# Attention scores: K in one tile per head, a sample block padded to 128 queries and 640 keys

## Chip, cores and metric

The kernel runs on one core of one Trainium2 chip. The metric is the device time of one execution in microseconds, as the median of several runs. The core's engines are TensorE (PE), VectorE (DVE), ScalarE (ACT), GpSimd (POOL) and SyncE (SP), which issues most DMAs.

## What is computed

One inference step of a two-layer streaming encoder: layer 0 is a Mamba-2 mixer with a SwiGLU feed-forward part, layer 1 a banded attention with another one. 1024 prompt frames and 64 sample frames go through both. The change lies in the attention of layer 1, 16 heads of 64:

```python
def band_attend(q, k, v, qpos, kpos, rel_bias):
    dist = jnp.clip(qpos[:, None] - kpos[None, :], -REL_CLIP, REL_CLIP) + REL_CLIP
    bias = rel_bias[:, dist].astype(jnp.float32)
    qc = qpos // CHUNK
    kc = kpos // CHUNK
    valid = (kpos[None, :] >= 0) & (kc[None, :] <= qc[:, None]) & (kc[None, :] >= qc[:, None] - BAND_CHUNKS)
    s = jnp.einsum('bqhd,bkhd->bhqk', q, k).astype(jnp.float32) * (ATT_HEAD_DIM ** -0.5) + bias
    s = jnp.where(valid, s, -jnp.inf)
    p = jax.nn.softmax(s, axis=-1).astype(v.dtype)
    return jnp.einsum('bhqk,bkhd->bqhd', p, v)
```

Chunks are of 64 frames, and a query sees its own chunk and the eight before it. The sample's 64 queries see 512 cached keys and their own 64.

## The kernel before

All activations lie transposed, features on the 128 partitions and the 1088 frames (1024 + 64) along the free dimension, in three slices of 384, 384 and 320 frames (`SL`). Matrix products are made in units: `unit` runs one 128-wide column block of weights over one slice, as 8 steps of three matmuls (`passes`, L454 to L456: weights and activations are each split into a high and a low float32r part). PE's order is the order in which the program emits its instructions. A `Stream` with a clock of its own, `st.t`, decides it: units advance the clock, and side tasks (the attention blocks among them) are let in between the quarters of a unit when their due times have come. The other engines' orders, SP's and POOL's DMA queues among them, are made by the compiler from priorities (`high_priority`) and dependences.

The attention goes by 8 pairs of heads (j = 0 to 7). For each pair, units make K, V and Q of each slice: `evk` (L1569), `evv` (L1623) and `evq` (L1589) take a unit's result from PSUM. K is scaled into `kf` and split for each of the two heads e into a tile whose one half of the partitions holds the high part and whose other half the low part (L1581 on ScalarE, L1582 on DVE). There are five buffers (`KBUF`) of 384 columns for each head, one for each slice of K; Q has two buffers for each of its four parts. A score is then two matmuls over 128 partitions, one with the high part of Q (L1675) and one with the low part (L1676).

`att_task(j, b)` handles block b of 9: blocks 0 to 7 are 128 prompt queries each against up to 640 keys (128 keys for block 0, 256, 384 and 512 for blocks 1 to 3, 640 from block 4 on), block 8 is the 64 sample queries against 576 keys. Stage A makes the scores. Since K lies in slices, they come in pieces (`pcs_`): 384+128 in block 3, 384+256 in blocks 4 and 7, 256+384 in block 5, 128+384+128 in block 6, and 512 (cached, `Ck`) + 64 in block 8. Pieces that fit together go into the same bank of a PSUM tile `S` of two banks. For each bank DVE then adds the bias and takes the row minimum of the negated scores (L1685), ScalarE makes the exponentials and their sum (L1690), and DVE divides (L1691, L1692). Stage B, later, transposes the probabilities by 128 keys on PE (L1707, tile `ptp`, in the same ring of two PSUM buffers as `S`) and copies them to `pT`, for head 0 on DVE and for head 1 on ScalarE (L1712; for block 8 the last 64 keys in a copy of their own, L1714). Stage C, `values` (L1728), multiplies V with them (L1746); after three blocks the output goes to `oscr` (L1754, L1755).

V of a slice is transposed by three 128-column matmuls in `v_task` (L1615) and copied to `Vn` (L1617, and L1619 for the sample's 64 rows). The bias of a pair is loaded for each head as a band of 128 by 640 (`load_bias`, L1555); POOL writes the mask into two of its corners (L1561, L1562). A unit waits until the blocks that read the oldest K, V or Q slices are emitted (`free_q`, L1766).

Of the kernel before, what the change touches and what calls it, by code (L numbers as in the profile page):

```python
# [374 lines left out]
def hybrid_kernel(  # L375
# [1148 lines left out]
    with ExitStack() as es:  # L1524
# [7 lines left out]
        def load_pair(j):  # L1532
            kqv[j] = dict(K={}, Q={}, V={})
# [32 lines left out]
        def k_tiles():  # L1566
            return [sb2.tile([P, 384], F32R, tag=f"K{e}", bufs=KBUF, name=f"K{e}") for e in range(2)]

        def evk(j):  # L1569
            d = kqv[j]  # L1570

            def f(s, p_):
# [5 lines left out]
                Kd = d["K"].get(s) or k_tiles()  # L1578
                for e in range(2):

                    A.copy(Kd[e][H2[e], :n], kf[H2[e], :n])  # L1581
                    V.tensor_tensor(Kd[e][H2[1 - e], :n], kf[H2[e], :n], Kd[e][H2[e], :n], op=ALU.subtract)  # L1582
                d["K"][s] = Kd
# [5 lines left out]
        def evq(j):  # L1589
            def f(s, p_):  # L1590
# [3 lines left out]
                kqv[j]["Q"][s] = Q  # L1594
                qf = sb2.tile([P, 384], F32, tag="kqv", bufs=2, name="qf")
# [14 lines left out]
        def v_task(j, s, vt):  # L1610
            Vn = kqv[j]["V"][s] = sb2.tile([P, 3, P], F32, tag="Vn", bufs=KBUF, name="Vn")
            pt = ax("vtp")
            for i in range(3):
                L = CHL[3 * s + i]
                PE.transpose(pt[:L, i * P:(i + 1) * P], vt[:, i * P:i * P + L], ident)  # L1615
            nf = 3 if s < 2 else 2
            V.tensor_copy(Vn[:, :nf, :], pt[:, :nf * P].rearrange("p (a b) -> p a b", b=P))  # L1617
            if s == 2:
                V.tensor_copy(Vn[:64, 2, :], pt[:64, 256:384])  # L1619
            yield 0.33, 0  # L1620
            v_done.append((j, s))

        def evv(j):  # L1623
            def f(s, p_):
# [6 lines left out]
                if s == 2:  # L1631
                    nc.sync.dma_start(vT_o[j * P:(j + 1) * P, 256:576], vt[:, :320])
# [5 lines left out]
        def att_task(j, b):  # L1638
# [9 lines left out]
            pcs_ = []  # L1648
            if b < 8:
                k0 = max(0, b - 4)  # L1650
                w_ = P * (b + 1 - k0)
                for t_ in range(3):
                    c0, c1 = max(k0, 3 * t_), min(b + 1, 3 * t_ + 3)
                    if c0 < c1:
                        pcs_.append((d["K"][t_], (c0 - 3 * t_) * P, (c1 - c0) * P))
            else:
                k0 = 0
                w_ = 576
                pcs_ = [(d["Ck"], 0, 512), (d["K"][2], 256, 64)]
            parts, bank, fill = [], 0, 0  # L1660
            for kd_, ko, fw in pcs_:
                if fill + fw > 512:
                    bank, fill = bank + 1, 0
                parts.append((bank, fill, kd_, ko, fw))
                fill += fw
            split = sum(p_[4] for p_ in parts if p_[0] == 0)
            nkt = (w_ + P - 1) // P
            sts = []
            for e in range(2):
                sp = psS.tile([P, 2, 512], F32, tag="S", name="S")  # L1670
                qs = slice(i * P, i * P + L)
                qh, ql = d["Q"][s][e]
                for bank, f0, kd_, ko, fw in parts:
                    dst = sp[:L, bank, f0:f0 + fw]
# [5 lines left out]
                brev = bt[:L, 0:w_][:, ::-1] if b < 8 else bt[:L, 64:640][:, ::-1]  # L1680

                low = TOP
                with tc.high_priority(ATP):
                    for pi, (f0, f1) in enumerate([(0, split)] + ([(split, w_)] if split < w_ else [])):
                        V.tensor_tensor_reduce(  # L1685
                            out=sc[:L, f0:f1], in0=sp[:L, pi, :f1 - f0], in1=brev[:, f0:f1],
                            scale=-1.0, scalar=low, op0=ALU.add, op1=ALU.min, accum_out=mx[:L, pi:pi + 1],
                        )
                        low = mx[:L, pi:pi + 1]
                    A.activation(sc[:L, :w_], sc[:L, :w_], AF.Exp, bias=low, scale=-1.0, accum_out=mx[:L, 3:4])  # L1690
                    V.reciprocal(mx[:L, 3:4], mx[:L, 3:4])  # L1691
# [293 lines left out]
```

## Time and profile before

| | us |
|---|---|
| median of 3 runs | 2992.34 |
| lowest, highest | 2991.45, 2995.91 |
| the profiled execution | 2995.14 |
| its span, first to last instruction | 2993.4 |
| mean granted PE clock | 0.993 |
| first score to last value matmul | 1659.1 to 2151.0 |

The profile is of one execution. In its lists, an instruction's row gives the start and the duration in us, the engine, the line of the kernel, the operation, what it writes and reads (tile names without buffer numbers), the shapes (for a matmul first the partitions and columns of the stationary operand, then those of the moving one), how many such instructions are merged in the row, and in brackets the idle time of the engine before it with what ended that. A row of the waits names who waited for whom, then the us in total, how often, and the longest. PE's matmuls are pipelined, and their ends are modelled. In a row with three durations these are the shortest, the median and the longest in ns.

### The profile page before, as it was taken

How to read it: one execution, taken by the hardware profiler on the slowest of the kernel's cores; microseconds unless marked ns; L12 is line 12 of the kernel's file. 1: busy time of each engine (PE TensorE's matmuls, PEld its weight loads, DVE VectorE, ACT ScalarE, POOL GpSimd, SP SyncE). 2: the span in 40 equal slices, each digit the busy share in tenths (PEclk: the TensorE clock that was granted, in tenths of full speed). 3: DMA queues.
4: the chain of work that ended last, by engine and by line, in shares of the span. 5: the costliest groups of instructions: out<-in, count | busy, mean ns of one | idle time of the engine just before them, and what ended most of it. 6: DMA issues, size and time to landing. Idle time of an engine off the chain costs nothing.

```text
span 2993.4 us, 56388 instructions
## 1 busy us (share of the span) xinstructions
PE 2935.9 (98%) x21626; PEld 2878.7 (96%) x21626; DVE 2039.4 (68%) x4471; ACT 1450.9 (48%) x2574; POOL 709.0 (24%) x821
## 2 busy tenths in 40 slices
PE   8899999999999999999999999999999999999999
PEld 7899999999999999999999899999999999999999
DVE  7788887876768554574557777777778655475544
ACT  6675666654453232244445566555654322244443
POOL 1233333330121433351111000000131343452111
PEclk9999999999999999999999999999999999999999
DMA  3333333334654222255655322222356222245654
GB/s 122 99 108 95 103 98 105 95 102 150 187 147 144 84 73 80 76 161 173 203 177 168 88 83 73 69 65 85 123 166 187 80 75 77 80 149 174 214 180 136
DMA packets 201550, 363.36 MB, mean 121 GB/s; under 512 B 20544, under 2 KB 149280, under 8 KB 201280
## 3 DMA queue, kind: packets, MB, share of 16 engines
q1 hardware_dynamic: 199488, 353.39, 38.1%
q0 software_dynamic: 1792, 6.36, 1.1%
q8 instruction: 170, 2.79, 0.4%
q14 instruction: 100, 0.82, 0.1%
HBM read 292.47 MB, written 62.74 MB: 119 GB/s over the span
## 4 chain that ended last, share of the span: by engine, by line
PE 83%; DVE 9%; DMA 4%; ACT 2%; issue 2%; POOL 0%; SPq 0%; DVEq 0%; ACTq 0%; POOLq 0%
PE px L1263 9%; PE px L1265 9%; PE px L1264 9%; PE mm L454 7%; PE mm L456 7%; PE mm L455 7%; PE po L1463 6%; PE po L1464 6%; PE po L1462 6%; PE mmx L455 3%; PE mmx L454 3%; PE mmx L456 3%; PE po L1746 2%; PE ptp L1707 1%; PE yp L884 1%
## 5 line engine op out<-in xcount | busy, mean ns | idle before, releaser
L454 PE MATMUL mm<-r,hl 128*128 128x384 f32 (+2 forms) x1664 | 557.9, 335 | 5.5 <-ACT BT L768 3.0
L456 PE MATMUL mm<-r,hl 128*128 128x384 f32 (+2 forms) x1664 | 540.3, 325 | 3.6 <-DVE hl L353 2.8
L455 PE MATMUL mm<-r,hl 128*128 128x384 f32 (+2 forms) x1664 | 539.2, 324 | 0.0
L341 DVE TENSOR_TENSOR hl<-raw,hl 128x1024 fp32r<-128x1024 f32 (+1 forms) x219 | 260.9, 1192 | 222.6 <-ACT hl L340 218.6
L1264 PE MATMUL px<-r,hl 128*128 128x288 f32 (+1 forms) x1184 | 347.6, 294 | 0.0
L454 PEld LDWEIGHTS mm<-r,hl 128*128 128x128 f32 x1664 | 316.1, 190 | 7.5 <-ACT BT L768 3.2
L456 PEld LDWEIGHTS mm<-r,hl 128*128 128x128 f32 x1664 | 315.2, 189 | 5.0 <-DVE hl L353 3.9
L455 PEld LDWEIGHTS mm<-r,hl 128*128 128x128 f32 x1664 | 316.5, 190 | 0.1
L1263 PE MATMUL px<-r,hl 128*128 128x288 f32 x1056 | 310.9, 294 | 0.0
L1265 PE MATMUL px<-r,hl 128*128 128x288 f32 x1056 | 310.7, 294 | 0.0
L340 ACT CAST hl<-raw 128x1024 fp32r<-128x1024 f32 (+1 forms) x219 | 219.9, 1005 | 177.5 <-PE po L1464 101.6
L480 POOL TENSOR_TENSOR ssum<-ssum,sq 128x256 f32<-128x256 f32 (+3 forms) x97 | 130.4, 1345 | 639.3 <-ACT sq L479 622.5
L1264 PEld LDWEIGHTS px<-r,hl 128*128 128x128 f32 x1184 | 222.6, 188 | 0.0
L1265 PE MATMUL px<-rx,hl 128*128 128x256 f32 x768 | 216.2, 282 | 4.5 <-DVE hl L341 4.5
L1263 PE MATMUL px<-rx,hl 128*128 128x256 f32 x768 | 216.7, 282 | 2.3 <-ACT hl L340 2.3
L1463 PE MATMUL po<-rx,hl 128*128 128x384 f32 (+1 forms) x624 | 201.6, 323 | 0.1
L1263 PEld LDWEIGHTS px<-r,hl 128*128 128x128 f32 x1056 | 198.4, 188 | 0.1
L1265 PEld LDWEIGHTS px<-r,hl 128*128 128x128 f32 x1056 | 198.3, 188 | 0.0
L1462 PE MATMUL po<-rx,hl 128*128 128x384 f32 (+1 forms) x608 | 197.4, 325 | 0.1
L1464 PE MATMUL po<-rx,hl 128*128 128x384 f32 (+1 forms) x608 | 196.5, 323 | 0.0
L1264 PE MATMUL px<-rx,hl 128*128 128x256 f32 x640 | 179.8, 281 | 0.0
L290 POOL TENSOR_TENSOR tt<-raw 128x512 f32<-128x512 f32 x40 | 56.0, 1399 | 439.3 <-DMA raw<-in_w_f_dram 362.9
(359 smaller groups left out, 8116.0 us busy)
## 6 DMA issues: line engine op xcount, KB each, us to landing
raw<-in_w_f_dram SPq DMA_DIRECT2D x154, 512.0 KB, 3.8
rx<-in_w_f_dram SPq DMA_DIRECT2D x54, 512.0 KB, 3.7
raw<-in_w_in_dram SPq DMA_DIRECT2D x40, 512.0 KB, 3.7
MT<-ascr SPq DMA_DIRECT2D x48, 384.0 KB, 3.8
sg<-hscr SPq DMA_DIRECT2D x88, 192.0 KB, 3.3
raw<-in_w_f_dram SPq DMA_DIRECT2D x44, 384.0 KB, 3.3
raw<-in_w_so_dram SPq DMA_DIRECT2D x32, 512.0 KB, 3.8
raw<-in_w_kv_dram SPq DMA_DIRECT2D x18, 512.0 KB, 3.5
```

The lines of the kernel that those rows point to most:

```text
L340: self.nc.scalar.copy(h, v)
L341: (eng or self.eng or self.nc.vector).tensor_tensor(lo, v, h, op=ALU.subtract)
L454: PE.matmul(ps[:, :n], h_, xh, start=(first and i == 0), stop=False)
L455: PE.matmul(ps[:, :n], h_, xl, start=False, stop=False)
L456: PE.matmul(ps[:, :n], l_, xh, start=False, stop=(last and i == nk - 1))
L480: (eng or G).tensor_tensor(ssum[:, :n], ssum[:, :n], q[:, :n], op=ALU.add)
L1263: PE.matmul(ps, wh, ah[:, k, :], start=(k == 0), stop=False)
L1264: PE.matmul(ps, wh, al[:, k, :], start=False, stop=False)
L1265: PE.matmul(ps, wl, ah[:, k, :], start=False, stop=(k == 3))
L1462: PE.matmul(ps[:, :n], wh, xh, start=(k == 0), stop=False)
L1463: PE.matmul(ps[:, :n], wh, xl, start=False, stop=False)
L1464: PE.matmul(ps[:, :n], wl, xh, start=False, stop=(k == FT - 1))
```

## The change

K of a pair lies in one tile of 9*128 columns per head, with two buffers. Its columns from 1088 on, Q's columns from 320 on in the last slice, and V's columns from 320 on in the last slice are filled with zeros by POOL. The scores of blocks 0 to 3 are made in one piece, those of blocks 4 to 7 in two halves of 320, and block 8 is taken with 128 queries and 640 keys, as 512 cached keys and a piece of 128. Its transposes, copies, reductions and exponentials are of full size; its values keep their 64 queries, but run over the 128 rows of the last piece. Block 8's bias is read from column 0 on, so that the existing mask corner covers the 64 keys that don't exist. The due times of block 8's stages are computed with 640 in place of 576. The diff:

```diff
@@ -1530,7 +1530,7 @@
         pos = {}
 
         def load_pair(j):
-            kqv[j] = dict(K={}, Q={}, V={})
+            kqv[j] = dict(K=set(), Kt=[], Q={}, V={})
 
         def load_side(j):
             d = kqv[j]
@@ -1563,9 +1563,6 @@
                 bias.append(bt)
             kqv[j]["bias"] = bias
 
-        def k_tiles():
-            return [sb2.tile([P, 384], F32R, tag=f"K{e}", bufs=KBUF, name=f"K{e}") for e in range(2)]
-
         def evk(j):
             d = kqv[j]
 
@@ -1575,12 +1572,15 @@
                 kf = sb2.tile([P, 384], F32, tag="kqv", bufs=2, name="kf")
                 with tc.high_priority(HIP):
                     V.tensor_tensor(kf[:, :n], p_[:, :n], rba[s][:, :n], op=ALU.mult)
-                Kd = d["K"].get(s) or k_tiles()
-                for e in range(2):
-
-                    A.copy(Kd[e][H2[e], :n], kf[H2[e], :n])
-                    V.tensor_tensor(Kd[e][H2[1 - e], :n], kf[H2[e], :n], Kd[e][H2[e], :n], op=ALU.subtract)
-                d["K"][s] = Kd
+                if not d["Kt"]:
+                    d["Kt"] = [sb2.tile([P, 9 * P], F32R, tag=f"K{e}", bufs=2, name=f"K{e}") for e in range(2)]
+                    for Kd in d["Kt"]:
+                        G.memset(Kd[:, T:].bitcast(F32), 0.0)
+                for e, Kd in enumerate(d["Kt"]):
+                    hi, lo = Kd[H2[e], 384 * s:384 * s + n], Kd[H2[1 - e], 384 * s:384 * s + n]
+                    A.copy(hi, kf[H2[e], :n])
+                    V.tensor_tensor(lo, kf[H2[e], :n], hi, op=ALU.subtract)
+                d["K"].add(s)
                 if s:
                     a_, b_, c_ = (128, 384, 0) if s == 1 else (0, 320, 256)
                     nc.sync.dma_start(kT_o[j * P:(j + 1) * P, c_:c_ + b_ - a_], kf[:, a_:b_])
@@ -1592,6 +1592,9 @@
 
                 Q = [[sb2.tile([P, 384], F32R, tag=f"Q{x}{e}", bufs=2, name=f"Q{x}{e}") for x in "hl"] for e in range(2)]
                 kqv[j]["Q"][s] = Q
+                if s == 2:
+                    for q_ in Q[0] + Q[1]:
+                        G.memset(q_[:, n:].bitcast(F32), 0.0)
                 qf = sb2.tile([P, 384], F32, tag="kqv", bufs=2, name="qf")
                 with tc.high_priority(HIP):
                     V.scalar_tensor_tensor(qf[:, :n], p_[:, :n], 0.125, rba[s][:, :n], op0=ALU.mult, op1=ALU.mult)
@@ -1611,12 +1614,8 @@
             Vn = kqv[j]["V"][s] = sb2.tile([P, 3, P], F32, tag="Vn", bufs=KBUF, name="Vn")
             pt = ax("vtp")
             for i in range(3):
-                L = CHL[3 * s + i]
-                PE.transpose(pt[:L, i * P:(i + 1) * P], vt[:, i * P:i * P + L], ident)
-            nf = 3 if s < 2 else 2
-            V.tensor_copy(Vn[:, :nf, :], pt[:, :nf * P].rearrange("p (a b) -> p a b", b=P))
-            if s == 2:
-                V.tensor_copy(Vn[:64, 2, :], pt[:64, 256:384])
+                PE.transpose(pt[:, i * P:(i + 1) * P], vt[:, i * P:(i + 1) * P], ident)
+            V.tensor_copy(Vn, pt[:, :3 * P].rearrange("p (a b) -> p a b", b=P))
             yield 0.33, 0
             v_done.append((j, s))
 
@@ -1629,6 +1628,7 @@
                 if s == 1:
                     nc.sync.dma_start(vT_o[j * P:(j + 1) * P, 0:256], vt[:, 128:384])
                 if s == 2:
+                    G.memset(vt[:, n:], 0.0)
                     nc.sync.dma_start(vT_o[j * P:(j + 1) * P, 256:576], vt[:, :320])
                 st.spawn(v_task(j, s, vt), 3.0 if j else 5.0)
             return f
@@ -1645,51 +1645,40 @@
             )
             L = CHL[b]
 
-            pcs_ = []
             if b < 8:
                 k0 = max(0, b - 4)
                 w_ = P * (b + 1 - k0)
-                for t_ in range(3):
-                    c0, c1 = max(k0, 3 * t_), min(b + 1, 3 * t_ + 3)
-                    if c0 < c1:
-                        pcs_.append((d["K"][t_], (c0 - 3 * t_) * P, (c1 - c0) * P))
+                half = w_ if w_ <= 512 else w_ // 2
+                parts = [(c_ // half, d["Kt"], k0 * P + c_, half) for c_ in range(0, w_, half)]
             else:
-                k0 = 0
-                w_ = 576
-                pcs_ = [(d["Ck"], 0, 512), (d["K"][2], 256, 64)]
-            parts, bank, fill = [], 0, 0
-            for kd_, ko, fw in pcs_:
-                if fill + fw > 512:
-                    bank, fill = bank + 1, 0
-                parts.append((bank, fill, kd_, ko, fw))
-                fill += fw
-            split = sum(p_[4] for p_ in parts if p_[0] == 0)
-            nkt = (w_ + P - 1) // P
+                k0, w_, half = 0, WIN, 512
+                parts = [(0, d["Ck"], 0, 512), (1, d["Kt"], 8 * P, P)]
+            nkt = w_ // P
             sts = []
             for e in range(2):
                 sp = psS.tile([P, 2, 512], F32, tag="S", name="S")
-                qs = slice(i * P, i * P + L)
+                qs = slice(i * P, (i + 1) * P)
                 qh, ql = d["Q"][s][e]
-                for bank, f0, kd_, ko, fw in parts:
-                    dst = sp[:L, bank, f0:f0 + fw]
+                for bank, kd_, ko, fw in parts:
+                    dst = sp[:, bank, :fw]
                     PE.matmul(dst, qh[:, qs], kd_[e][:, ko:ko + fw], start=True, stop=False)
                     PE.matmul(dst, ql[:, qs], kd_[e][:, ko:ko + fw], start=False, stop=True)
                 sc = late["sb3"].tile([P, WIN], F32, tag="sc", bufs=4, name="sc")
                 mx = late["sb3"].tile([P, 4], F32, tag="mx", bufs=4, name="mx")
                 bt = d["bias"][e]
-                brev = bt[:L, 0:w_][:, ::-1] if b < 8 else bt[:L, 64:640][:, ::-1]
+                brev = bt[:, 0:w_][:, ::-1]
 
                 low = TOP
                 with tc.high_priority(ATP):
-                    for pi, (f0, f1) in enumerate([(0, split)] + ([(split, w_)] if split < w_ else [])):
+                    for pi, (f0, f1) in enumerate([(0, half)] + ([(half, w_)] if half < w_ else [])):
                         V.tensor_tensor_reduce(
-                            out=sc[:L, f0:f1], in0=sp[:L, pi, :f1 - f0], in1=brev[:, f0:f1],
-                            scale=-1.0, scalar=low, op0=ALU.add, op1=ALU.min, accum_out=mx[:L, pi:pi + 1],
+                            out=sc[:, f0:f1], in0=sp[:, pi, :f1 - f0], in1=brev[:, f0:f1],
+                            scale=-1.0, scalar=low, op0=ALU.add, op1=ALU.min, accum_out=mx[:, pi:pi + 1],
                         )
-                        low = mx[:L, pi:pi + 1]
-                    A.activation(sc[:L, :w_], sc[:L, :w_], AF.Exp, bias=low, scale=-1.0, accum_out=mx[:L, 3:4])
-                    V.reciprocal(mx[:L, 3:4], mx[:L, 3:4])
-                    V.tensor_scalar(sc[:L, :w_], sc[:L, :w_], mx[:L, 3:4], None, op0=ALU.mult)
+                        low = mx[:, pi:pi + 1]
+                    A.activation(sc[:, :w_], sc[:, :w_], AF.Exp, bias=low, scale=-1.0, accum_out=mx[:, 3:4])
+                    V.reciprocal(mx[:, 3:4], mx[:, 3:4])
+                    V.tensor_scalar(sc[:, :w_], sc[:, :w_], mx[:, 3:4], None, op0=ALU.mult)
                 sts.append(sc)
             cur["A"] = seqn + 1
             cur["t"] = st.t + 1.1 * w_ / 640 + GAP_A
@@ -1703,15 +1692,11 @@
                 pT = late["sb3"].tile([P, 5, P], F32, tag="pT", bufs=6, name="pT")
                 pt = psS.tile([P, 2, 512], F32, tag="S", name="ptp").rearrange("p a b -> p (a b)")
                 for kt in range(nkt):
-                    kw = min(P, w_ - kt * P)
-                    PE.transpose(pt[:kw, kt * P:kt * P + L], sts[e][:L, kt * P:kt * P + kw], ident[:L, :L])
+                    PE.transpose(pt[:, kt * P:(kt + 1) * P], sts[e][:, kt * P:(kt + 1) * P], ident)
                 ptv = pt[:, :640].rearrange("p (a b) -> p a b", b=P)
-                nfull = w_ // P
                 cpf = A.copy if e else V.tensor_copy
                 with tc.high_priority(ATP):
-                    cpf(pT[:, :nfull, :L], ptv[:, :nfull, :L])
-                    if nfull < nkt:
-                        cpf(pT[:64, nfull, :L], ptv[:64, nfull, :L])
+                    cpf(pT[:, :nkt, :L], ptv[:, :nkt, :L])
                 PTs.append(pT)
             cur["B"] = seqn + 1
             cost += 1.1 * w_ / 640
@@ -1735,16 +1720,15 @@
                     pos["po"] = ax("po")
                 po = pos["po"]
                 for kt in range(nkt):
-                    kw = min(P, w_ - kt * P)
                     for e in range(2):
                         if 3 * s + i < 8:
                             vs = d["V"][(k0 + kt) // 3][:, (k0 + kt) % 3, 64 * e:64 * e + 64]
                         elif kt < 4:
                             vs = d["Cv"][:, kt, 64 * e:64 * e + 64]
                         else:
-                            vs = d["V"][2][:64, 2, 64 * e:64 * e + 64]
+                            vs = d["V"][2][:, 2, 64 * e:64 * e + 64]
                         PE.matmul(
-                            po[64 * e:64 * e + 64, i * P:i * P + L], vs, PTs[e][:kw, kt, :L],
+                            po[64 * e:64 * e + 64, i * P:i * P + L], vs, PTs[e][:, kt, :L],
                             start=(kt == 0), stop=(kt == nkt - 1),
                         )
                 if i == 2:
@@ -1808,7 +1792,6 @@
                 if s and w is wv:
                     W.put()
 
-        kqv[0]["K"][2] = k_tiles()
         units(W.get(), 1, evk, (0, 1))
         W.put()
         st.wait_for(lambda: 2 in done)
```

## The prediction

> **What bounds the kernel now.** I read the page's engine shares first, then the engines over the attention stage alone, then what TensorE (PE) waited for there, and last the order of instructions in one head pair.
>
> ```profile
> PE 2935.9 (98%) x21626; PEld 2878.7 (96%) x21626; DVE 2039.4 (68%) x4471; ACT 1450.9 (48%) x2574; POOL 709.0 (24%) x821
> ```
>
> ```profile
> 1655.00:2150.00 495.00, 480.30 (x3873) 455.15 (x3871) 385.69 (x1212) 294.85 (x730) 5.32 (x31) 1.00 0.26 77
> ```
>
> ```profile
> PE ptp L1707 <- DVE mx L1685: 4.8, 9, 1.9
> PE S L1675 <- DVE pT L1712: 4.4, 11, 0.6
> ```
>
> The first line says that PE is busy for 98% of the whole span. The second is the stretch 1655 to 2150 us, in which all scores of the change lie: after the length come the busy times of PE, weight load, DVE, ACT and POOL, then the granted clock, 1.00. PE works 480.30 of 495.00 us, so it bounds this stage too; DVE has 385.69, 78%, and POOL almost nothing. The last two lines are the waits in that stretch that involve the edited lines: 4.8 us in all of the transposes for the score reduction, and 4.4 us of the scores for a copy of transposed probabilities. Whatever the change does to other stages is at most a shift of memory addresses. So the sum is made of PE time in the score, transpose and value steps of 8 head pairs, and of what these waits make of it. Times of starts matter here, not durations: PE's matmuls overlap, and what one costs is the time until the next starts.
>
> **Scores of block 3 (keys 0 to 511), from 384+128 to one 512.** Per head (e = 0, 1) the block issues a high and a low matmul for each piece.
>
> ```profile
> 1801.02 0.34 PE L1675 MATMUL S<-K,Qh 128*128 128x384 f32 x1
> ...
> 1802.11 0.39 PE L454 MATMUL mm<-r,hl 128*128 128x384 f32 x1
> 1802.34 0.34 PE L455 MATMUL mm<-r,hl 128*128 128x384 f32 x1
> ```
>
> The eight matmuls take 1802.11 - 1801.02 = 1.09 us, and the one after them lasts 0.23 instead of 0.17 us (0.17 is the step of a 384 in the middle of a unit), so 1.15 us. Four matmuls of 512 come instead, priced by the sample block's:
>
> ```profile
> 1775.86 0.45 PE L1675 MATMUL S<-Ck,Qh 128*64 128x512 f32 x1 [0.37 <-DVE pT L1712]
> ...
> 1776.47 0.42 PE L1675 MATMUL S<-Ck,Qh 128*64 128x512 f32 x1
> 1776.72 0.39 PE L1676 MATMUL S<-Ck,Ql 128*64 128x512 f32 x1
> 1776.95 0.19 PE L1675 MATMUL S<-K,Qh 128*64 128x64 f32 x1
> ...
> 1777.04 0.55 PE L1615 MATMUL vtp<-ident,vt 128*128 128x128 f32 x3
> ```
>
> A 512 steps 1776.95 - 1776.72 = 0.23 us, so four take 0.92: a gain of 0.23 us per pair. For this same step the Trainium skill (TensorE: Matmul & The Clock Gate, section Back-to-back issue gap) gives about 131 ns per 512-column matmul in a sustained stream; by it the four would take 0.52 us and the gain of this block would be 0.63 us per pair, an estimate from that page. The rows above, 0.23 and 0.25 us, do not agree with it, and the sum goes by the rows.
>
> **Scores of block 6, from 128+384+128 to 320+320.**
>
> ```profile
> 1819.85 0.22 PE L1675 MATMUL S<-K,Qh 128*128 128x128 f32 x1
> ...
> 1821.21 0.22 PE L1675 MATMUL S<-K,Qh 128*128 128x128 f32 x1
> ...
> 1821.38 0.39 PE L454 MATMUL mm<-r,hl 128*128 128x384 f32 x1
> ```
>
> ```profile
> 1782.35 0.31 PE L456 MATMUL mm<-r,hl 128*128 128x320 f32 x1
> ...
> 1783.67 0.31 PE L456 MATMUL mm<-r,hl 128*128 128x320 f32 x1
> ```
>
> Now 1821.38 - 1819.85 = 1.53 us, and again about 0.06 in the matmul behind it: 1.59. A 320 steps (1783.67 - 1782.35)/9 = 0.147 us, as the second fence holds the first and last of ten of them, so eight take 1.18: a gain of 0.41 us per pair. Blocks 4, 5 and 7 go from 384+256 to 320+320, the same number of matmuls and of columns, and I cost them at nothing; blocks 0 to 2 stay as they are.
>
> **The sample block (8): scores, transposes, values.** The first 512 after the wait stays. Each head's two 64-column pieces, 1777.04 - 1776.95 = 0.09 us, become two of 128, which took 1821.38 - 1821.21 = 0.17 us at the end of block 6; and what follows a pair of 128 steps up to 0.06 us longer. So two heads cost 0.16 to 0.28 us more; I take 0.20. For the transposes:
>
> ```profile
> 1783.91 0.82 PE L1707 MATMUL ptp<-ident,sc 64*128 64x64 f32 x10
> 1784.65 0.42 PE L454 MATMUL mm<-r,hl 128*128 128x320 f32 x1
> ```
>
> ```profile
> 1804.08 0.34 PE L456 MATMUL mm<-r,hl 128*128 128x384 f32 x1
> 1804.25 0.82 PE L1707 MATMUL ptp<-ident,sc 128*128 128x128 f32 x6
> 1804.82 0.42 PE L454 MATMUL mm<-r,hl 128*128 128x384 f32 x1
> ```
>
> ```profile
> 2145.71 1.31 PE L1707 MATMUL ptp<-ident,sc 128*128 128x128 f32 x10
> ```
>
> From the last unit matmul before to the first after, ten half-size transposes take 1784.65 - 1783.67 = 0.98 us; six full ones take 1804.82 - 1804.08 = 0.74. Ten full ones last 1.31 where six last 0.82, so four more are up to 0.49, and ten would be 1.23 us at most; with the bare column ratio they would be near 1.15. I take 0.20 us more per pair, between 0.17 and 0.25.
>
> ```profile
> 1788.84 0.64 PE L1746 MATMUL po<-pT,Cv 128*64 128x64 f32 x16
> 1789.40 0.33 PE L1746 MATMUL po<-pT,Vn 64*64 64x64 f32 x4
> 1789.67 0.44 PE L1707 MATMUL ptp<-ident,sc 128*128 128x128 f32 x2
> ```
>
> The values keep 64 queries. Today 16 matmuls take 0.56 us and the 4 of half height 0.27. Made full height they should go at the rate of the 16, 0.035 each, so 0.14: 0.13 us less. How they hand over to the next instruction isn't in the trace, so the bounds are 0 and 0.13 and I take 0.10.
>
> **The sum on PE** is -0.23 - 0.41 + 0.20 + 0.20 - 0.10 = -0.34 us per pair, -2.7 us over 8.
>
> **What the wait does with it.** Block 6's scores stand ahead of one of the waits of the first section. Its rows:
>
> ```profile
> 1821.18 0.55 DVE L1602 TENSOR_TENSOR Ql<-qf,Qh 64x384 fp32r<-64x384 f32 x1 [0.58 <-ACT Qh L1600]
> ...
> 1821.66 0.68 DVE L1685 CUSTOM_DVE_ANT_0 sc<-S,bias 128x512 f32<-128x512 f32 x1
> ...
> 1823.53 0.71 PE L1707 MATMUL ptp<-ident,sc 128*128 128x128 f32 x5
> ...
> 1824.25 0.08 DVE L1685 DVE_READ_ACCUMULATOR2_ANT mx<- 128x1 f32 x1
> ...
> 1824.48 0.30 PE L1707 MATMUL ptp<-ident,sc 128*128 128x128 f32 x1 [0.24 <-DVE mx L1685]
> ```
>
> The score tiles and the transposed tiles share one ring of two. So the second head's transposes of block 5 need the slot of block 6's second score tile, which is free only when DVE has read it, at 1824.33; PE was there 0.24 us earlier. DVE's chain did not start with the scores but with the Q eviction: it idled 0.58 us for ScalarE's Qh, made Ql, and only then took the first reduction. If DVE keeps this order, its chain ends where it ends now, PE arrives 0.41 us sooner and waits 0.65 instead of 0.24. The reductions themselves cost the same: 512+128 columns or 320+320. This is my forecast, for the six pairs 1 to 6 whose blocks stand in this order: 6 x 0.41 = 2.5 us of the 2.7 are lost, and -0.2 us stays. The bounds of this term are 0 lost, and 2.5 lost.
>
> **What I cost at nothing.** DVE's and ScalarE's work for block 8 grows by 64 columns, and two copies become one:
>
> ```profile
> L1685 DVE CUSTOM_DVE_ANT_0 sc<-S,bias,mx 64x64 f32<-64x64 f32 x2 | 0.5, 272 | 0.0
> ...
> L1685 DVE CUSTOM_DVE_ANT_0 sc<-S,bias,mx 128x128 f32<-128x128 f32 x2 | 0.7, 350 | 0.1
> L1619 DVE COPY Vn<-vtp 64x128 f32<-64x128 f32 x1 | 0.3, 286 | 0.0
> ```
>
> Two reductions go from 272 to 350 ns, +0.16 us per pair, and the second copy of V, 0.29 us, goes into the first. That cancels, and the cover is PE's own work, since DVE idles a fifth of the stage. If the cover were gone it would be 0.16 us a pair, 1.3 us. Seven zero fills per pair come to POOL:
>
> ```profile
> L471 POOL MEMSET ssum<- x13: 148/178/342, 3.3 to 2821.7; 128x96 f32 x8, 128x64 f32 x5
> ```
>
> At the 0.18 us median of these fills, which have the same shape or half as much again, that is 1.2 us per pair on an engine with 5.32 us of work in 495. A rule that speaks against them stands in the Trainium skill (SBUF — State Buffer, section SBUF: two separate sides): a POOL instruction holds a port pair that some DVE instructions need, and the loser waits it out. By that rule it would be at most 1.2 us of DVE time per pair; no run here shows it. K in one tile of two slots, in place of slices in five: the tile of pair 2 overwrites that of pair 0.
>
> ```profile
> 1714.53 0.22 PE L1676 MATMUL S<-K,Ql 128*64 128x64 f32 x1
> ```
>
> ```profile
> 1743.63 1.05 ACT L1581 CAST K<-kf 64x384 fp32r<-64x384 f32 x2 [0.80 <-DVE kf L1577]
> ```
>
> The last reader of pair 0's K is at 1714.53 and the first writer of pair 2's at 1743.63, so the new wait is over 29 us before it could bite. Behind it would stand ScalarE's casts and the Q evictions, but they never meet it. The Q, V and K fills likewise wait for slots that the evictions beside them wait for already. DMAs stay as they are.
>
> **Rivals.** *The gain comes through.* The first half of block 6 is complete after two of its matmuls instead of four, early enough for its 0.5 us reduction to go into DVE's 0.58 us hole. Then DVE's chain ends half a microsecond sooner, the 0.41 us stays and the 0.24 us wait goes as well: -2.7 - 6 x 0.24 = -4.1 us. For it: the hole is there. Against it: today's first half, done by about 1820.6, didn't go in either. 2988.2 us.
>
> *A late mask: slower.* Each pair's first reduction already waits for POOL's mask fill:
>
> ```profile
> 1778.24 0.81 SPq L1560 DMA_DIRECT2D bias<-in_rbrow_dram x2
> ```
>
> ```profile
> 1781.76 0.14 POOL L1561 MEMSET bias<- 64x64 f32 x1 [61.29 <-DMA bias<-in_rbrow_dram]
> 1781.93 0.29 DVE L1685 CUSTOM_DVE_ANT_0 sc<-S,bias 128x128 f32<-128x128 f32 x1 [1.09 <-POOL bias L1561]
> ```
>
> POOL works in order. If the compiler puts new fills ahead of this one, and one of them waits for its slot, the mask is late, and DVE, with evictions queued behind that reduction, stands still. PE's next use of this softmax is the transposes at 1789.67, 7.7 us after the reduction starts and about 6 us after it could be ready; so it decides from 6 us of delay, and each microsecond beyond costs 7 us over the 7 pairs: from +6 up, 2998.5 us at one microsecond more. Against it: the slots that the fills wait for come free for the evictions at about the same time.
>
> *Block 8's longer chain.* If its larger reductions and transposes move a ring wait in each pair by 0.2 to 0.5 us beyond the sum, and block 6 gains nothing, it is +1.5 to +4 us, near 2995. *No effect at all*, the pieces compiling to the same instructions, can't be: the shapes are in the instructions.
>
> **How the numbers follow.** The profiled execution took 2995.14 us with a span of 2993.4, 1.7 around it, and the median of the runs is 2992.34. From its own time the forecast is 2994.9; from the median, 2992.1, which I give. Chances: forecast 0.46; gain comes through 0.22; block 8's chain 0.14; late mask, or another reordering of the planner's queues of that size, 0.18. 0.2%, 6 us, is about what a measurement of this kernel can tell from no change. Only the late mask and the edge of block 8's chain are slower than that, 0.21; of the gain case the part in which the 0.37 us wait at block 8's scores goes too (another 3 us) is faster, 0.11; the rest, 0.68, is the same. The range reaches from 2986, the gain case with some of that wait, to 2999, the late mask at its lower end.
>
> **What would show it.** Right: line for line no 128-column score piece but in blocks 0 and 8, 448 score matmuls in place of 512, block 6 in about 1.2 us, and the wait of the second transposes near 0.65 us in six pairs. If that wait is 0.24 or less, the gain case holds. A reduction that waits for POOL by several microseconds shows the late mask. The forecast is wrong if PE's idle time in this stage changes by more than 5 us, or if PE time outside it moves.

## The result

The changed kernel takes 2984.42 us (median of 8 runs, 2982.39 to 2989.59) where the kernel before takes 2992.48 (8 runs, 2988.63 to 2995.91). The ratio is 0.9975, with a 95% interval of 0.9966 to 0.9984: about 8 us faster. The forecast was 2992.1 us, a change too small to tell from none; the result lies 1.6 us under the lower end of its range and 3.8 us under the rival that had the sign right.

### The profile after

The profiled execution of the changed kernel took 2984.73 us, with a span of 2983.0. First the engine shares of its page, then the attention stage over the engines (columns as before: length, busy time and instructions of PE, weight load, DVE, ACT and POOL, granted clock, DMA share, GB/s), then the two waits of PE in that stage.

```profile
PE 2926.5 (98%) x21562; PEld 2871.3 (96%) x21562; DVE 2041.4 (68%) x4455; ACT 1452.9 (49%) x2566; POOL 713.5 (24%) x877
```

```profile
1649.00:2139.50 490.50, 478.07 (x3809) 455.99 (x3807) 385.89 (x1196) 296.44 (x722) 14.30 (x83) 0.99 0.27 77
```

```profile
PE S L1664 <- DVE pT L1699: 5.0, 11, 0.6
PE ptp L1695 <- DVE mx L1674: 2.0, 3, 0.9
```

The edit did what it says: 64 matmuls fewer (21626 to 21562), which is 8 pairs by 4 in block 3 and 4 in block 6. The stage is still PE's: 478.07 of 490.50 us. POOL grew from 5.32 to 14.30 us of work, DVE not at all (385.69 to 385.89). And one wait has gone: the transposes waited 9 times and 4.8 us for a reduction, now 3 times and 2.0 us. The wait of the scores for a copy has not gone; it rose from 4.4 to 5.0 us.

To keep the stage's edges out of it, I took the time between the same two unit matmuls of each execution, the 11550th and the 13200th (counted from 0) of those that are not attention's; below this is the attention's window. It takes 484.7 us before and 479.7 after, so 5.0 us of the two profiles' difference lie in the attention. A second profile of each (below) gives 485.2 and 478.4, so 6.8. PE's granted clock falls to a half for single stretches of 3.4 us, and the two windows of each kernel hold three of these: one (1703.7) and two before, two (1689.0 and 1699.2) and one after. Each can cost 1.7 us of PE, an estimate from its length, so the mean, 5.9, says more than either pair. All attention matmul groups stand at the same places among the unit matmuls in both kernels: PE's order did not change.

Now the rows that answer to those of the prediction. Block 3's scores, and behind them the unit matmuls, on PE's timeline of the changed kernel (start, duration, engine, line, operation):

```profile
1796.46 0.39 PE L1664 MATMUL S<-K,Qh 128*128 128x512 f32 x1
...
1797.38 0.33 PE L454 MATMUL mm<-r,hl 128*128 128x384 f32 x1
1797.55 0.34 PE L455 MATMUL mm<-r,hl 128*128 128x384 f32 x1
```

1797.38 - 1796.46 = 0.92 us where it was 1.09, and the matmul behind them steps 0.17 where it was 0.23: together -0.23, as costed. Block 6:

```profile
1815.04 0.31 PE L1664 MATMUL S<-K,Qh 128*128 128x320 f32 x1
...
1816.21 0.34 PE L454 MATMUL mm<-r,hl 128*128 128x384 f32 x1
1816.38 0.34 PE L455 MATMUL mm<-r,hl 128*128 128x384 f32 x1
```

1.17 us where it was 1.53, and again 0.06 behind it: -0.42. What the forecast had wrong stands in DVE's timeline at the same place:

```profile
1815.24 0.56 DVE L1600 SCALAR_TENSOR_TENSOR qf<-mm,rbf 128x384 f32<-128x384 f32 x1 [1.36 <-PE mm L456]
1815.82 0.49 DVE L1674 CUSTOM_DVE_ANT_0 sc<-S,bias 128x320 f32<-128x320 f32 x1
...
1816.83 0.48 DVE L1674 CUSTOM_DVE_ANT_0 sc<-S,bias 128x320 f32<-128x320 f32 x1
...
1817.24 0.55 DVE L1605 TENSOR_TENSOR Ql<-qf,Qh 64x384 fp32r<-64x384 f32 x1
1817.71 0.53 DVE L1674 CUSTOM_DVE_ANT_0 sc<-S,bias,mx 128x320 f32<-128x320 f32 x1
1818.18 0.07 DVE L1674 DVE_READ_ACCUMULATOR2_ANT mx<- 128x1 f32 x1
```

Before, DVE idled 0.58 us after qf, made Ql, and only then took the first reduction of block 6. Now three of the four 320-column reductions stand ahead of Ql in its queue, the first at the end of qf, and the idle time is gone. The read of the last one's result, at 1818.18, frees the second score tile before PE starts the transposes, whose second five need its slot:

```profile
1818.33 1.25 PE L1695 MATMUL ptp<-ident,sc 128*128 128x128 f32 x10
1819.34 0.42 PE L454 MATMUL mm<-r,hl 128*128 128x384 f32 x1
```

All ten transposes run in one go, 1819.34 - 1818.33 = 1.01 us. In the kernel before the ten began at 1823.53, the second five after 0.24 us of idle time, and what came behind them was

```profile
1824.97 0.42 PE L454 MATMUL mm<-r,hl 128*128 128x384 f32 x1
```

so 1.44 us. A wait that the profile shows as 0.24 us of idle time cost 0.43. The first five's 0.71 us include the end of their pipeline, which the next five would have covered.

The sample block: its scores, transposes and values in the changed kernel.

```profile
1770.26 0.47 PE L1664 MATMUL S<-Ck,Qh 128*128 128x512 f32 x1 [0.46 <-DVE pT L1699]
...
1771.65 0.52 PE L1617 MATMUL vtp<-ident,vt 128*128 128x128 f32 x3
```

```profile
1778.26 0.31 PE L456 MATMUL mm<-r,hl 128*128 128x320 f32 x1
1778.40 1.25 PE L1695 MATMUL ptp<-ident,sc 128*128 128x128 f32 x10
1779.41 0.39 PE L454 MATMUL mm<-r,hl 128*128 128x320 f32 x1
```

```profile
1783.59 0.63 PE L1730 MATMUL po<-pT,Cv 128*64 128x64 f32 x16
1784.05 0.29 PE L1730 MATMUL po<-pT,Vn 128*64 128x64 f32 x4
1784.27 0.44 PE L1695 MATMUL ptp<-ident,sc 128*128 128x128 f32 x2
```

Scores 1.39 us where they took 1.18: +0.21. From the last unit matmul to the first after the transposes 1779.41 - 1778.26 = 1.15 where it was 0.98: +0.17. Values 1784.27 - 1783.59 = 0.68 where they took 0.83: -0.15. And the wait ahead of the scores is 0.46 us where it was 0.37.

### The profile page after: what moved, and what is told of

It is laid out like the page before. It is cut to its first block, busy times and chain, and to the rows that moved or that the text cites. A ratio compares the mean times of both kernels' runs of the same rounds, so it can differ in the third digit from the quotient of the medians.

```text
span 2983.0 us, 56344 instructions
## 1 busy us (share of the span) xinstructions
PE 2926.5 (98%) x21562; PEld 2871.3 (96%) x21562; DVE 2041.4 (68%) x4455; ACT 1452.9 (49%) x2566; POOL 713.5 (24%) x877
## 4 chain that ended last, share of the span: by engine, by line
PE 87%; DVE 6%; DMA 3%; ACT 2%; issue 1%; POOL 0%; SPq 0%; DVEq 0%; ACTq 0%; POOLq 0%
PE px L1263 9%; PE px L1264 9%; PE px L1265 9%; PE mm L456 8%; PE mm L454 8%; PE mm L455 7%; PE po L1463 6%; PE po L1464 6%; PE po L1462 6%; PE mmx L455 4%; PE mmx L454 4%; PE mmx L456 4%; PE po L1730 2%; PE ptp L1695 2%; PE S L1664 1%
```

## The experiments

Theory A: the gain is that of the rival "the gain comes through"; block 6's first half is ready early enough for the build to put its reduction ahead of Ql in DVE's queue, and with that the ring wait goes. Theory B, at first: most of the 8 us are chance or come from elsewhere, since the two first profiles differ by 5.9 us already ahead of the attention, where both kernels run the same program. Later experiments take the parts of the gain, and of the padding, one by one.

### The changed kernel again, and the kernel before against itself

No edit in either.

> The changed kernel once more. Theory A (all of the effect lies in the attention stage; the part of the first profiles' difference that lies ahead of it, 5.9 us at the 1640th microsecond, is chance of the single executions, from stretches of half PE clock at the start): over many executions 4 to 5 us under the kernel before, near 2988, and in the profile the first value transposes' neighbourhood anywhere from 1639 to 1646 us. Theory B (something ahead of the attention is steadily faster too): 8 us under, near 2984, and the start of attention near 1639 us again.

> The kernel before, unchanged, against itself: ratio 1.000, and how far it strays from that is the noise of such a comparison. Theory A: its profile's start of attention may fall anywhere between 1639 and 1646 us. Theory B: near 1645 us again.

The changed kernel: 2983.72 us (11 runs), ratio 0.9977 [0.9969, 0.9986] to the kernel before at 2990.4 on that chip, 6.7 us under it. The kernel before as its own rival: 2989.16 us (11 runs), ratio 0.9999 [0.9991, 1.0008]. So the gain is the change's, though bigger than the 4 to 5 us that A expected. Its place follows from the two profiles: the attention's window 485.2 and 478.4 us, 6.8 of it there. The start of the window follows no kernel: 1648.1 and 1640.4 us before, 1642.2 and 1643.1 after, against what B expected. What lies ahead of it is chance, as the first 210 us of three executions show: first the kernel before, then the changed one, then the second profile of the kernel before.

```profile
0.00:210.00 210.00, 188.06 (x1212) 178.05 (x1213) 167.08 (x418) 132.84 (x206) 53.34 (x110) 0.94 0.36 112
```

```profile
0.00:210.00 210.00, 189.54 (x1256) 179.30 (x1257) 170.50 (x429) 137.40 (x212) 56.40 (x114) 0.97 0.37 115
```

```profile
0.00:210.00 210.00, 190.33 (x1248) 180.49 (x1249) 169.98 (x426) 136.58 (x210) 55.73 (x114) 0.96 0.36 115
```

The granted clock, third column from the end, is 0.94 in the first and 0.97 and 0.96 in the others. In these 210 us PE has stretches at half clock that fall differently in each execution. The 1600th unit matmul starts at 268.6 us in the first profile of before, and between 262.0 and 264.6 in the eleven other profiles of this study, the second of before (263.0) among them. The 2995.14 us of the profile before the change were a long single execution of that kernel.

### The old pieces in the changed kernel

Blocks 3 to 7 are split at the 384-column slices again, with everything else of the change kept.

```diff
-parts = [(c_ // half, d["Kt"], k0 * P + c_, half) for c_ in range(0, w_, half)]
+for t_ in range(3):
+    fw = P * (min(b + 1, 3 * t_ + 3) - max(k0, 3 * t_))
+    ...
+        parts.append((bank, fill, d["Kt"], k0 * P + c_, fw))
```

> The changed kernel (one K tile, padded sample block) with the score pieces and reductions of blocks 3 to 7 as wide as before (384+128, 384+256, 256+384, 128+384+128, 384+256). Theory A: blocks 3 and 6 lose 0.23 and 0.41 us per pair again, the ring wait of 0.24 us comes back in six pairs, and block 8 keeps its extra 0.3 us: 2 to 3 us over the kernel before, near 2995. Theory B: still 1 us or more under it. Theory C (one K tile or its fills cost or gain something themselves): more than 4 us off the kernel before in either direction.

2992.87 us (11 runs), ratio 1.0009 [1.0000, 1.0018]: 2.5 us over the kernel before, 9 over the changed one. The whole gain hangs on the pieces; the padding by itself brings none and by these medians costs a little. By the rows above the padding should cost 0.21 + 0.17 - 0.15 + 0.09 = 0.32 us a pair, 2.6 us. The attention's window of this one profile is 486.4 us, 1.2 and 1.7 over before's 485.2 and 484.7: runs, rows and window lean the same way.

### The pieces without the padding

The kernel before, with K in one tile and scores in one piece or two halves, but the sample block left at 64 queries and 576 keys, and no fills.

```diff
-for t_ in range(3):
-    ...
-        pcs_.append((d["K"][t_], (c0 - 3 * t_) * P, (c1 - c0) * P))
+split = w_ if w_ <= 512 else w_ // 2
+parts = [(c_ // split, 0, d["Kt"], k0 * P + c_, split) for c_ in range(0, w_, split)]
```

> One K tile per head and one piece or two halves, but the sample block with 64 queries and 576 keys as before and no zero fills. Theory A: blocks 3 and 6 gain 0.64 us per pair, the ring wait goes, and block 8 costs nothing extra: 6 to 7 us under the kernel before, near 2986, 2 to 2.5 us under the changed one. Theory B: 10 us under the kernel before. A theory that the padding is what gains: not below the kernel before by more than 3 us.

2980.16 us (5 runs), ratio 0.9967 [0.9955, 0.998]: 10 us under the kernel before, where 6 to 7 were expected. This half of the change alone is better than all of it.

### Ql put back ahead of the reductions

The changed kernel with an order of issue, and no wait, between Ql and the first head's reductions of block 6: each of the two comes behind one of the two instructions that make Ql, so that Ql stands first again, as the forecast assumed.

```diff
-V.tensor_tensor(ql[H2[e], :n], qf[H2[e], :n], qh[H2[e], :n], op=ALU.subtract)
+lastql.append(V.tensor_tensor(ql[H2[e], :n], qf[H2[e], :n], qh[H2[e], :n], op=ALU.subtract))
...
+if b == 6 and e == 0:
+    tc.add_manual_dep(red.ins, lastql[pi].ins.name, ORD, reason="order")
```

> The changed kernel, but in block 6 DVE is told to issue the subtractions that make Ql ahead of head 0's two reductions, as it stood before the change. Theory A (block 6's gain and the vanished ring wait hang on DVE taking the reductions first): the second transposes of block 5 wait 0.65 us or more again in six pairs, 0.8 to 1 us with their restart, so 5 to 6 us over the changed kernel, near 2989. Theory B (the shorter reductions and the earlier scores alone do it): waits under 0.3 us, within 2 us of the changed kernel.

2989.81 us (11 runs) against 2989.99, ratio 0.9995 [0.9986, 1.0004]: no gain. DVE's timeline and PE's, at the place of the rows above:

```profile
1817.16 0.55 DVE L1610 TENSOR_TENSOR Ql<-qf,Qh 64x384 fp32r<-64x384 f32 x1 [0.58 <-ACT Qh L1608]
...
1819.14 0.55 DVE L1679 CUSTOM_DVE_ANT_0 sc<-S,bias,mx 128x320 f32<-128x320 f32 x1
1819.62 0.55 DVE L1679 CUSTOM_DVE_ANT_0 sc<-S,bias,mx 128x320 f32<-128x320 f32 x1
```

```profile
1818.93 0.34 PE L458 MATMUL mm<-r,hl 128*128 128x384 f32 x1
1819.76 1.31 PE L1702 MATMUL ptp<-ident,sc 128*128 128x128 f32 x10 [0.49 <-DVE mx L1679]
1820.83 0.42 PE L456 MATMUL mm<-r,hl 128*128 128x384 f32 x1
```

The 0.58 us of idle time are back, and PE waits 0.49 us ahead of all ten transposes. The order is not the old one in every place: the second halves of both heads now come last, at 1819.14 and 1819.62, so the first tile too is still unread when PE comes. From the last unit matmul before to the first after it is 1820.83 - 1818.93 = 1.90 us, against 1819.34 - 1818.14 = 1.20 in the changed kernel (its matmul ahead of the ten starts at 1818.14) and 1824.97 - 1823.35 = 1.62 before (there it starts at 1823.35). So the order of a few DVE instructions decides whether block 6's 0.42 us arrive: with Ql first, 0.28 of them go into the wait, and the sample block's longer wait takes 0.09 more. By the medians the change is then worth 0.2 us, with an interval from 4.2 us faster to 1.2 slower; that this is the figure of the forecast to the tenth is luck.

### Block 6 alone with the old pieces

The changed kernel; only block 6 is split in 128+384+128 again, by the lines of the old pieces above.

> The changed kernel, block 6 alone with its old pieces 128+384+128 and reductions of 512 and 128. Theory A: the matmuls cost 0.37 to 0.41 us per pair again, and the ring wait costs 0.43 us in five pairs and 0.8 in one as in the kernel before: 6 us over the changed kernel, near 2990, so that block 6 carries most of the effect. Theory B (the gain is spread over blocks 3 to 7): 2 to 3 us over it.

2992.07 us (11 runs), ratio 1.0006 [0.9997, 1.0014]. This one block carries the whole gain. On PE's timeline the ring wait is back as it was; in the list of waits of the stage, the transposes' is back too, and the scores' has grown from 5.0 us to 5.4.

```profile
1819.79 0.71 PE L1707 MATMUL ptp<-ident,sc 128*128 128x128 f32 x5
1820.74 0.74 PE L1707 MATMUL ptp<-ident,sc 128*128 128x128 f32 x5 [0.24 <-DVE mx L1686]
```

```profile
PE S L1676 <- DVE pT L1711: 5.4, 10, 0.9
PE ptp L1707 <- DVE mx L1686: 5.0, 9, 1.9
```

Against the changed kernel that is 8 x 0.42 = 3.4 us of PE, 3.0 us of ring waits (five pairs of 0.43 and 0.8 in pair 6), a new wait of block 1's scores in pair 3, 0.89 us, and a longer one in pair 2, 0.79 where the changed kernel has 0.59: 7.5 us. The first pair adds 0.8 to 0.9 (below). The median lies 7.7 and 8.4 us over the two of the changed kernel, which ran on other chips.

### Keys padded, queries not

The changed kernel with the sample block at 64 queries again; its keys stay at 640.

```diff
-if s == 2:
-    for q_ in Q[0] + Q[1]:
-        G.memset(q_[:, n:].bitcast(F32), 0.0)
...
-qs = slice(i * P, (i + 1) * P)
+qs = slice(i * P, i * P + L)
...
-PE.transpose(pt[:, kt * P:(kt + 1) * P], sts[e][:, kt * P:(kt + 1) * P], ident)
+PE.transpose(pt[:, kt * P:kt * P + L], sts[e][:L, kt * P:(kt + 1) * P], ident[:L, :L])
```

> The changed kernel, but block 8 keeps its 64 queries against the padded 640 keys, and Q gets no zero fill. Theory A (128 query columns cost the transposes 0.26 us per pair and the wait at block 8's scores 0.09 us): 2 us under the changed kernel, near 2981.5, with that wait back at 0.37 us. Theory B (the padded keys are what costs): within 1 us of the changed kernel.

2977.8 us (5 runs), ratio 0.9959 [0.9946, 0.9971]: 12 us under the kernel before and 6 under the changed kernel's median (2983.72), where 2 under it were expected. The ten transposes step 0.76 us again (1.01 in the changed kernel). From the last unit matmul before them to the first after them it is 1.00 us against 1.15, so 0.15 of it is a gain. The scores take 1.22 us (1.39), and the wait ahead of them has its old length:

```profile
1767.14 0.45 PE L1661 MATMUL S<-Ck,Qh 128*64 128x512 f32 x1 [0.37 <-DVE pT L1696]
```

0.15 + 0.17 + 0.09 = 0.41 us a pair, 3.3 us over 8; the attention's window of this profile is 475.2 us, 3.2 to 4.5 under the two of the changed kernel. The rest of the 6 us is not taken apart; a wait of block 1's scores in pair 2, 0.59 us in the changed kernel, isn't there.

### Ql on POOL, in the kernel before

If only the ring wait counts, taking Ql from DVE should bring its part of the gain without any new pieces.

```diff
-V.tensor_tensor(ql[H2[e], :n], qf[H2[e], :n], qh[H2[e], :n], op=ALU.subtract)
+G.tensor_tensor(ql[H2[e], :n], qf[H2[e], :n], qh[H2[e], :n], op=ALU.subtract)
```

> The kernel before, with Ql made by POOL in place of DVE. Theory A (in the kernel before, the ring wait comes from DVE's reductions of block 6 standing behind Ql): the wait of the second transposes goes in the six pairs, 3 us under the kernel before, near 2987.5, with the score pieces as they were. Theory B (the wait comes from the 512-wide reduction or from the late scores themselves): the wait stays near 0.24 us and the time is within 1.5 us of the kernel before, or higher if POOL is late with Ql.

2987.6 us (11 runs), ratio 0.9992 [0.9983, 1.0001]: 2.4 us under the kernel before by the medians, near the 3 that A expected, but the interval reaches from 5 us faster to no change. On PE's timeline the ten transposes run through, 1821.77 - 1820.76 = 1.01 us; the list of waits shows what took the place of the gap.

```profile
1820.76 1.25 PE L1707 MATMUL ptp<-ident,sc 128*128 128x128 f32 x10
1821.77 0.42 PE L454 MATMUL mm<-r,hl 128*128 128x384 f32 x1
```

```profile
PE S L1675 <- DVE pT L1712: 5.3, 15, 0.6
PE ptp L1707 <- DVE mx L1685: 1.2, 2, 0.7
PE ptp L1707 <- DVE pT L1712: 1.3, 2, 0.9
PE S L1675 <- ACT pT L1712: 1.2, 2, 0.7
```

The transposes' wait for the reduction fell from 4.8 us to 1.2. But in the same stretch, 1660 to 2140 us, the scores now wait 15 times and 5.3 us for DVE's copy where they waited 10 times and 4.1 us, and twice for ScalarE's, 1.2 us, which they didn't before; the transposes wait 1.3 us for a copy where they waited 0.4. Together these are 9.0 us, where they were 9.3. The attention's window of this one profile is 486.3 us, no shorter than before's 484.7 and 485.2. A was right on the wait; that the time follows from it isn't shown, since in the profile the ring's wait moved to other places.

### The two best again

The keys-only kernel and the kernel without padding, side by side on another chip, without an edit.

> The kernel with 64 queries and 640 padded keys in block 8 once more, on one chip with the one without any padding. Theory A (the padded keys cost nearly nothing, the padded queries cost 3 us): 10 to 12 us under the kernel before, and within 1.5 us of the one without padding. Theory B (the padded keys gain something): 2 us or more under the one without padding again.

> One K tile, one piece or two halves, block 8 unpadded, once more beside the one with padded keys. Theory A: 10 to 11 us under the kernel before, within 1.5 us of the other. Theory B: 2 us or more over the other again.

2977.86 us, ratio 0.9961 [0.9948, 0.9975], and 2979.3 us, ratio 0.9966 [0.9954, 0.9979] (5 runs each, before 2990.86). Both beat both kernels of the case; between the two there is no difference that these runs can tell. (From one transpose of V to the same one of the next pair, the six middle pairs take 61.56 to 61.64 us with the padded keys and 61.63 to 62.26 without, so a small gain of the padded keys is possible.) So of the padding, that of the keys costs nothing that can be measured, and that of the queries costs all of it.

## Why the prediction was wrong, point by point

**What bounds the stage.** Right. PE stays at 97% of it, DVE's and POOL's busy times did not matter, and the change is worth what PE's starts and waits make of it.

**The PE sum.** Right, term by term, in the steady pairs: block 3 -0.23 costed and -0.23 measured, block 6 -0.41 and -0.42, the sample block's scores +0.20 and +0.21, its transposes +0.20 and +0.17, its values -0.10 and -0.15. The sum was -0.34 and is -0.42 us a pair, -3.4 us over 8. Here the row decided against the page: by the 131 ns of the Trainium skill (TensorE: Matmul & The Clock Gate, section Back-to-back issue gap) block 3 would have gained 0.63 us, an estimate from that page. It gained 0.23.

**What the wait does with it: the step that failed.** "If DVE keeps this order, its chain ends where it ends now" was a condition, and it was false: in the changed kernel three of block 6's four reductions stand ahead of Ql, and the 0.24 us of ring wait, which was to grow to 0.65, is gone in the six pairs. The kernel with Ql put back shows that the working behind the condition was nearly right: its wait is 0.49 us and its gain 0.2 us. The profile had shown the hole of 0.58 us and a first half of block 6 that would be complete two matmuls earlier, and I weighed that down with "today's first half, done by about 1820.6, didn't go in either". That was no argument. The order of DVE's queue is made when the program is built: in the kernel before, that first half was done as the hole opened, at 1820.6, and DVE idled through it all the same. The forecast moved the matmuls without asking again what the queue behind them would look like. That the order turned round is in the traces; what in the build turned it is not. The rival had the mechanism, at 0.22, and only its size too small: from the start of block 6's scores to the last reduction's read, DVE's chain takes 3.21 us where it took 4.48, so it ends 1.27 us sooner and not half a microsecond.

**The rival's price, mis-sized.** It priced the lost wait at its idle time, 6 x 0.24 = 1.5 us, though in pair 6 the row shows 0.67. Start to start it was 0.43 us in five pairs and 0.8 in the sixth, 3.0 us. With the sum of -3.4 that is -6.4 us; the longer wait ahead of the sample block's scores, 8 x 0.09, gives back 0.7. So -5.7 us in the steady state; two profiles of each kernel show -5.0 to -6.8 in the window, and the medians -6.7 and -8.1. Not in this sum is the first pair, whose matmuls start crowded: from block 6's first score to block 7's it took 5.46 and 5.53 us in the two profiles of before and takes 4.27 in both of the changed kernel, 1.2 to 1.3 us less, of which the sum holds 0.42. The order on DVE decides this as well: it is 5.63 us with the new pieces and Ql put back, and 4.42 with the old pieces and Ql on POOL. (A half-clock stretch covers the end of it in each profile of before and in the one with Ql put back, so a part of the 0.8 that are left may be the clock's.)

**Block 8's longer chain.** Its price was named for this rival, 0.2 to 0.5 us a pair, and is 0.09 us in the wait ahead of the scores; the rival's other half, that block 6 gains nothing, did not come. The wait goes with the queries (0.37 us with 64 of them). Two things changed with 128 queries, as the weight loads of the sample block's scores show, first in the changed kernel, then before (nanoseconds, least, median, most):

```profile
L1664 PEld LDWEIGHTS S<-Ck,Qh x16: 186/188/192, 1708.6 to 2133.0; 128*128 128x128 f32 x16
```

```profile
L1675 PEld LDWEIGHTS S<-Ck,Qh x16: 132/135/138, 1713.4 to 2143.8; 128*64 128x64 f32 x16
```

The load takes 0.053 us longer. And ahead of each pair's first one the changed kernel's weight queue shows a semaphore instruction of 0.051 us: it waits for DVE's copy there, and the load itself now waits for a semaphore of POOL, which fills Q. The kernel with padded keys alone, without that fill, has neither that instruction nor the longer load. How the 0.09 us divide between the two stays open.

**The late mask.** It did not happen. POOL's fills stood in the places that the rival feared, but none held up the mask, as the changed kernel's POOL timeline shows around one pair's sample block:

```profile
1771.19 0.15 POOL L1578 MEMSET K<- 128x64 f32 x1 [43.52 <-PE S L1665]
1771.88 0.15 POOL L1578 MEMSET K<- 128x64 f32 x1 [0.54 <-PE S L1665]
1775.58 0.18 POOL L1561 MEMSET bias<- 64x64 f32 x1 [3.54 <-DMA bias<-in_rbrow_dram]
```

The fill of K does wait for its slot, 43.52 us, with the mask behind it. But it had the slot at 1771.19, and the mask then waited 3.54 us more for its own DMA; the fill would have to be that much later to matter. (The price named for this rival was also added up wrong: 2992.1 and 7 us are 2999.1, not 2998.5.) The reductions' whole wait for the mask fell. The line of it in the list of what they wait for, before and then after (us, times):

```profile
  POOL bias L1561: 6.2, 7
```

```profile
  POOL bias L1561: 1.2, 3
```

**What was costed at nothing.** K in one tile: right, pair 2's first cast into its tile starts at 1738.32, 29 us after the tile had come free for its fill (1709.57). The fills: right; 9 us more POOL work left DVE's busy time within 0.2 us, so of the Trainium skill's rule on the shared ports (SBUF — State Buffer, section SBUF: two separate sides), by which DVE would lose up to 1.2 us a pair by the prediction's estimate, nothing shows here.

**The numbers.** By the medians the order of issue alone is worth 5.4 to 6.1 us, between the one with Ql put back and the two of the changed kernel. The rival's 2988.2 missed the result by 3.8: 1.5 by the ring wait's price, 0.7 by the PE sum, less the 0.7 of the sample block's wait. Of the 2.3 that remain, the first pair has at most 0.8; the rest stays open, and the medians 6.7 and 8.1 differ by nearly as much. The range's lower end of 2986 hung on the sample block's wait of 0.37 us going away; it grew. The base of three runs, 2992.34, lies 1.5 to 3.2 us over the later medians of the kernel before (2989.16 to 2990.86), so the lower end stood 6.3 us under the base, and the repeated measurement is 6.7 us under its own.

## What to carry to other kernels

When a step moves, redo the queue of every engine that reads its result: its order is made when the program is built, and here an operand that comes 0.3 us earlier went with instructions turned round; that order was worth more than the matmuls saved. Price a wait by the starts on both sides of it, with and without the wait, and not by the idle time that the row shows. And take a change of several parts apart: here the split of the scores carried the whole gain, and the zeros for the queries took 4 to 6 us of it back.

## What the runs showed that I had not expected

A wait in the middle of ten transposes costs 0.43 us start to start where its row shows 0.24 of idle time, since the row counts from the modelled end of the fifth, and that end of the pipeline is uncovered as well.

Block 6's pieces were worth 8 us, over twice their PE time, because with them went the ring wait, a part of the first pair and, in one pair, a wait of scores. And the same ring wait, removed by moving Ql to POOL, left the stage as long as it was in the one profile, since it came back at other places; the runs leave a gain of 0 to 5 us open. Which places a ring of two will wait at could not be read from the profile of before.

In the first 210 us the granted clock was 0.94, 0.97 and 0.96 in three executions, and the 1600th unit matmul came at 262.0 to 268.6 us. So single executions of one kernel differ by 5.6 us there, which is nearly the size of the result. The half-clock stretches lasted 3.4 us or multiples of it, up to 10.2, and came to 23.9, 13.7 and 17.1 us up to that matmul. At half speed the first execution loses 5.1 and 3.4 us more by them than the other two, an estimate, of 6.6 and 5.6; the rest stays open. The Trainium skill (TensorE: Matmul & The Clock Gate, Part 1: The HAM clock gate) tells of a window of about 3.4 us that runs free of the kernel's start, and that the number of slow matmuls varies from run to run; the traces agree.
